# Finishing the last stream in two column runs, gates through tanh, and paired norm additions in a fused layer kernel on eight cores

## The chip, the cores and the metric

The kernel runs on all eight cores of one Trainium2 chip. Cores 0 to 3 are one die, cores 4 to 7 the other. Each core works on one prompt of the batch, with one eighth of the single-token samples, and no core waits for another, so the device time is the time of the slowest core. The metric is that time in microseconds (us). Lower is better.

A program on all eight cores also has a slow state in some of its executions: the cores of one die, sometimes of both, show a lower granted clock (0.81 to 0.98 on them in the slow runs recorded here) and the time is longer (1593 to 1875 us). Engine names in the profile: PE is TensorE, PEld its weight loads, DVE is VectorE, ACT is ScalarE, POOL is GpSimd, SP issues DMA transfers.

## The reference

The reference is one layer of a hybrid decoder, with RMS norms before and after each part:

```
x = x + 0.5 * rms(swiglu1(rms(x)))          # d_model 1024, hidden 2816
h = rms(x);  u = h @ w_in                   # the mixer
  branch A:  (a_b * conv3(a_c * a_x)) @ w_out_a
  branch B:  c = conv4(b_x) + bias
             r = sigmoid(c @ w_r + b_r);  i = sigmoid(c @ w_i + b_i)   # the recurrent gates
             a = exp(-8 * r * softplus(-lambda))
             u = sqrt(1 - a*a) * (i * c);  h_t = a_t * h_(t-1) + u_t
             (gelu(b_gate) * h) @ w_out_b
x = x + rms((sigmoid(g_a)*A + sigmoid(g_b)*B) @ w_o)
x = x + 0.5 * rms(swiglu2(rms(x)))          # the last norm, then the output
```

It returns x for the prompt and the samples, and the new convolution and recurrent states.

## The kernel before

A core keeps features on the 128 partitions and tokens along the columns. Its 2080 tokens are five *streams*. All weights pass through a ring in SBUF once for each group of streams: the first two streams share a pass, the other three have one each.

```python
SIZES = [418, 418, 416, 414, 414]
GROUPS = [[0, 1], [2], [3], [4]]
BUFSET = [0, 1, 2, 0, 1]          # three sets of stream buffers
```

The kernel is written as operations with reads, writes and a priority, and a list scheduler in the program simulates five engines and fixes each engine's order of instructions when the program is built. The priorities come from long tables of fitted numbers, one start and one end for each weight unit of each group. Whoever edits one operation therefore moves many.

```python
def at(g, u, cls, st, fn, *a):
    which, off = CLASSES[cls]
    S.prio = nominal[g][u][which] + off + (LAGS[u] * st.pos if st is not None else 0.0)
    ...
```

A post-norm needs the mean square over features. ScalarE squares each 128-row block as it comes from PSUM, VectorE adds up the squares, and a matmul with a matrix of ones sums over the partitions. The last stream's final norm is then a tail after the last weight matmul:

```python
def rms_finish(ps, n):
    rv = newf()
    act(rv[0:n], ps[0:n], AF.Ln, n, [ps] + DP, [rv], bias=EPS, psum=True)
    act(rv[0:n], rv[0:n], AF.Exp, n, [rv], [rv], scale=-0.5)
    return rv

def final_norm(st, acc):
    s, n, o, m = st.s, st.n, st.o, st.m
    rv = rms_finish(acc, m)
    events = []
    for oc in range(KC):                              # KC = 8 blocks of 128 features
        yv = O32[s][:, oc * m:(oc + 1) * m]           # dense output buffer
        ...
        tt(tv[0:m], y32[s][:, oc, 0:m], rv[0:m], ALU.mult, ...)
        tt(yv, xs_view(st, oc, o, n), tv[0:m], ALU.add, ...)
        if st.last and (oc + 1) % 2 == 0:
            events.append(store_y(st, oc - 1, oc + 1))    # (ACC_TAIL is False)
    return events
```

`xs_view` is the stream's running x in SBUF, `y32` the output of the last product, `O32` a dense fp32 buffer over the hidden activations that are no longer needed. `store_y` sends two blocks, 2 x 414 fp32 values in a row on each partition, in one transfer. The recurrent gates of the mixer take nine ScalarE activations for each stream and block:

```python
act(r, pzr, AF.Exp, scale=-1.0, bias=dcol(0, j));  act(b, pzi, AF.Exp, scale=-1.0, bias=dcol(1, j))
act(r, r, AF.Ln, bias=1.0);  act(r, r, AF.Exp, scale=-1.0);  act(a, r, AF.Exp, scale=dcol(2, j))
act(r, r, AF.Exp, scale=dcol(5, j));  act(r, r, AF.Ln, bias=1.0, scale=-1.0)
act(b, b, AF.Ln, bias=1.0);  stt(r, r, 0.5, b, ALU.mult, ALU.subtract);  act(r, r, AF.Exp)
tt(cb, r, cb, ALU.mult)                      # (slices, reads and writes cut)
```

In the head, `keep_warm(n)` issues matmuls of 128 columns on the ones matrix into a scratch bank; the last 50 of them are the *filler*.

## Time and profile before

| | before |
|---|---|
| median of the first three runs | 1564.75 us (1563.51 to 1565.17) |
| spans of the eight cores in the profiled run | 1557.1 to 1563.7 us |
| TensorE busy, slowest core | 98% |
| last weight matmul to the end, median core | 14.96 us |

The page's first part, kernel before, gives busy time, share of the span and instruction count of each engine:

```profile
span 1563.7 us, 27199 instructions; the slowest of 8 cores (1557.1 to 1563.7 us)
PE 1532.3 (98%) x8771; PEld 847.6 (54%) x8771; DVE 813.1 (52%) x1535; ACT 771.8 (49%) x1367; POOL 247.7 (16%) x470
```

TensorE is the limit, and other engines matter only where TensorE stands still. The view of waits says for what it stood still (total, number of times, longest; the first three lines):

```profile
PE P L662 <- ACT qp L676: 5.9, 5, 3.1
PE P L662 <- DVE qp L680: 3.9, 2, 2.8
PE P L662 <- DVE xs L704: 2.6, 2, 2.2
```

The wait of 2.8 us on `DVE qp` is the third stream's first pre-norm sum, near 78 us. The 2.2 us on `DVE xs` is near 1233 us, in the last stream's mixer. The same two places in the view of windows of core 0; PE's busy time and matmul count come first after the window's length, and the granted clock is the third number from the end:

```profile
76.00:81.00 5.00, 2.17 (x12) 1.07 (x11) 2.88 (x5) 2.58 (x6) 1.05 (x2) 0.95 0.94 176
81.00:84.00 3.00, 3.00 (x10) 1.27 (x9) 0.69 (x2) 2.74 (x4) 0.00 (x0) 0.51 1.03 190
1232.00:1236.00 4.00, 2.43 (x9) 1.17 (x10) 3.42 (x10) 2.83 (x6) 0.42 (x1) 0.78 0.75 258
1236.00:1240.00 4.00, 4.00 (x20) 2.03 (x19) 1.97 (x5) 2.59 (x6) 0.53 (x1) 0.79 0.36 128
```

The tail, in the timeline of core 0 (start, duration, engine, operation; in brackets the idle time before it and what ended it):

```profile
1545.84 2.97 PE L662 MATMUL P<-big,wring 128*128 128x414 bf16 x16
1548.90 0.52 ACT L676 ACTIVATE qp<-P 128x414 bf16<-128x414 f32 x1 [2.64 <-PE P L662]
1549.56 0.34 PE L662 MATMUL P<-qp,ones 128*128 128x414 bf16 x1 [0.58 <-ACT qp L676]
1550.62 0.55 ACT L676 ACTIVATE fp<-fp 128x414 f32<-128x414 f32 x1
1551.27 0.59 DVE L680 TENSOR_TENSOR fp<-hy,fp 128x414 f32<-128x414 f32 x1 [5.01 <-ACT fp L676]
1551.96 0.59 DVE L680 TENSOR_TENSOR big<-xs,fp 128x414 f32<-128x414 f32 x1
...
1560.32 0.59 DVE L680 TENSOR_TENSOR big<-xs,fp 128x414 f32<-128x414 f32 x1
```

The last weight matmul ends at 1548.81. Sixteen VectorE operations run from 1551.27 to 1560.91, and the rest to 1563.7 is the last of four transfers. The DMA view of that stretch:

```profile
GB/s 0 0 0 0 0 0 0 0 0 0 0 0 0 0 0 0 99 397 397 166 0 0 108 389 406 157 0 0 116 397 397 149 0 0 116 397 414 133 0 0
DMA packets 576, 1.70 MB, mean 106 GB/s; under 512 B 64, under 2 KB 64, under 8 KB 576
yout<-big SPq DMA_DIRECT2D x4, 414.0 KB, 2.5
```

Four bursts near 400 GB/s, each over long before the next, so only the last one is waited for.

### The profile page before, as it was taken

The page shows a single profiled execution, that of the slowest core. Times are in us where ns is not written, and L with a number is a line of the kernel's source. Part 1 is how long each engine was busy: PE and PEld are TensorE (multiplying, and loading weights), DVE is VectorE, ACT ScalarE, POOL GpSimd, SP SyncE. Part 2 cuts the span into 40 slices and gives each one's busy share as a digit, 9 for nine tenths or more (in the row PEclk, how much of TensorE's full clock was granted, in tenths as well). Part 3 has the DMA queues.
Part 4 walks back from the last instruction along what each step waited for, and adds up shares of the span by engine and source line. Part 5 has one row for each costly group of instructions (what it writes and reads, how often), then busy time and mean ns, then how long its engine had stood idle before and what let it go on. Part 6 is the DMA issues. An engine that isn't in the chain of part 4 may idle for free.

```text
span 1563.7 us, 27199 instructions; the slowest of 8 cores (1557.1 to 1563.7 us)
## 1 busy us (share of the span) xinstructions
PE 1532.3 (98%) x8771; PEld 847.6 (54%) x8771; DVE 813.1 (52%) x1535; ACT 771.8 (49%) x1367; POOL 247.7 (16%) x470
## 2 busy tenths in 40 slices
PE   8999999999999999999999999999999999999996
PEld 5555555555555555555555555555555555555553
DVE  3232108988787467722127452356567887661143
ACT  3221136788877567411154332446575678451222
POOL 1001111011111111011111122222221111112220
PEclk9999999999999999999999999999999999999998
DMA  9889767766877775898766776655575555545653
GB/s 192 227 193 205 155 159 179 200 146 190 203 162 191 201 201 145 200 203 188 180 178 189 249 247 202 198 181 172 183 254 202 163 174 186 205 170 181 199 185 106
DMA packets 81002, 294.88 MB, mean 189 GB/s; under 512 B 9696, under 2 KB 9824, under 8 KB 80864
## 3 DMA queue, kind: packets, MB, share of 16 engines
q0 software_dynamic: 60704, 223.12, 56.2%
q1 hardware_dynamic: 20160, 70.02, 11.9%
q8 instruction: 74, 1.21, 0.3%
q14 instruction: 64, 0.52, 0.1%
HBM read 284.76 MB, written 64.45 MB: 223 GB/s over the span
## 4 chain that ended last, share of the span: by engine, by line
PE 93%; DVE 3%; DMA 2%; issue 1%; ACT 1%; DVEq 0%; POOL 0%; SPq 0%; ACTq 0%; POOLq 0%
PE P L662 93%; DMA xs<-xin 1%; DMA wring<-wsc 1%; DVE fp L694 1%; DVE fp L680 1%; ACT fp L676 0%; DVE big L680 0%; ACT L676 0%; DVE xs L704 0%; DVE fp L699 0%; DVE fp L688 0%; DVEq L1143 0%; DVE qp L680 0%; ACT qp L676 0%; DVE xs L680 0%
## 5 line engine op out<-in xcount | busy, mean ns | idle before, releaser
L662 PE MATMUL P<-hy,wring 128*128 128x414 bf16 (+4 forms) x6080 | 1101.3, 339 | 5.7 <-DVE xs L704 2.2
L662 PEld LDWEIGHTS P<-hy,wring 128*128 128x128 bf16 x6080 | 591.0, 97 | 487.8 <-issue 14.4
L676 ACT ACTIVATE fp<-P 128x414 f32<-128x414 f32 (+4 forms) x529 | 267.7, 516 | 625.1 <-PE P L662 613.2
L662 PE MATMUL P<-big,wring 128*128 128x414 bf16 (+3 forms) x2400 | 442.8, 338 | 0.3 <-DVE xs L704 0.3
L680 DVE TENSOR_TENSOR big<-P,fp 128x414 bf16<-128x414 f32 (+3 forms) x260 | 151.2, 588 | 403.7 <-PE P L662 379.6
L662 PEld LDWEIGHTS P<-big,wring 128*128 128x128 bf16 x2400 | 233.2, 97 | 189.3 <-issue 1.0
L734 POOL DMA_DIRECT2D wring<-wsc x344 | 182.9, 532 | 802.5 <-PE P L662 786.1
L680 DVE TENSOR_TENSOR fp<-fp 128x414 f32<-128x414 f32 (+3 forms) x215 | 122.5, 572 | 131.2 <-ACT fp L676 124.3
L734 POOL DMA_DIRECT2D wring<-wall x117 | 62.0, 533 | 470.8 <-PE P L662 446.5
L676 ACT ACTIVATE fp<-fp 128x418 f32<-128x418 f32 (+2 forms) x230 | 121.1, 546 | 13.3 <-DVE fp L694 4.0
L676 ACT ACT_TABLE_LOAD x84 | 107.8, 1283 | 28.9 <-PE P L662 19.2
L694 DVE SCALAR_TENSOR_TENSOR fp<-P,par_sb,fp 128x418 f32<-128x418 f32 (+3 forms) x120 | 77.4, 646 | 24.9 <-ACT fp L676 16.9
L694 DVE SCALAR_TENSOR_TENSOR hy<-xs,par_sb,fp 128x414 bf16<-128x414 f32 (+3 forms) x120 | 69.1, 646 | 21.0 <-ACT fp L676 21.0
L694 DVE SCALAR_TENSOR_TENSOR fp<-fp,P 128x414 f32<-128x414 f32 (+3 forms) x80 | 45.4, 580 | 51.6 <-PE P L662 47.5
L676 ACT ACTIVATE fp<-xs 128x414 f32<-128x414 f32 (+3 forms) x104 | 55.1, 545 | 28.2 <-DVE xs L680 27.9
L694 DVE SCALAR_TENSOR_TENSOR fp<-fp,par_sb 128x402 f32<-128x402 f32 (+4 forms) x80 | 51.5, 644 | 7.2
L680 DVE TENSOR_TENSOR fp<-hy,fp 128x414 f32<-128x414 f32 (+3 forms) x80 | 46.7, 584 | 15.6 <-ACT fp L676 15.6
L676 ACT ACTIVATE fp<-fp,dpar 128x418 f32<-128x418 f32 (+2 forms) x80 | 51.1, 639 | 7.2 <-DVE fp L694 1.7
L676 ACT ACTIVATE hy<-P,dpar 128x414 f32<-128x414 f32 (+3 forms) x80 | 48.6, 607 | 7.5 <-ACT fp L676 0.7
L680 DVE TENSOR_TENSOR xs<-xs,fp 128x414 f32<-128x414 f32 (+3 forms) x80 | 47.1, 588 | 6.3 <-DVE fp L680 0.8
L676 ACT ACTIVATE fp<-P,dpar 128x418 f32<-128x418 f32 (+2 forms) x80 | 44.5, 604 | 10.6 <-PE P L662 8.9
L699 DVE TENSOR_TENSOR_SCAN fp<-fp,CAR 128x418 f32<-128x418 f32 (+3 forms) x40 | 43.1, 1076 | 3.8
(44 smaller groups left out, 379.4 us busy)
## 6 DMA issues: line engine op xcount, KB each, us to landing
wring<-wsc POOLq DMA_DIRECT2D x244, 512.0 KB, 4.7
wring<-wall POOLq DMA_DIRECT2D x83, 512.0 KB, 8.2
wsc<-wring SPq DMA_DIRECT2D x83, 512.0 KB, 7.0
wring<-wsc POOLq DMA_DIRECT2D x96, 352.0 KB, 4.1
wring<-wall POOLq DMA_DIRECT2D x32, 352.0 KB, 6.8
wsc<-wring SPq DMA_DIRECT2D x32, 352.0 KB, 5.6
xs<-xin SPq DMA_DIRECT2D x4, 828.0 KB, 7.5
xs<-xin SPq DMA_DIRECT2D x4, 418.0 KB, 6.4
```

What stands on the lines that cost most here:

```text
L662: ins = e.matmul(o, ev(lhs_list[k]), ev(rhs_list[k]), start=(start and k == 0), stop=(stop and k == nk - 1))
L676: return S.op("act", lambda e: e.activation(out=ev(out), in_=ev(in_), func=func, **kw), reads, writes, dur, tbl=TBL.get(func), prio=prio)
L680: return S.op("dve", lambda e: e.tensor_tensor(out=ev(out), in0=ev(in0), in1=ev(in1), op=op), reads, writes, 0.153 + n / 960.0, prio=prio)
L694: return S.op("dve", lambda e: e.scalar_tensor_tensor(out=ev(out), in0=ev(in0), scalar=scalar, in1=ev(in1), op0=op0, op1=op1), reads, writ ...
L699: return S.op("dve", lambda e: e.tensor_tensor_scan(out=ev(out), data0=ev(d0), data1=ev(d1), initial=init, op0=ALU.mult, op1=ALU.add), rea ...
L734: S.dma("pool", lambda e: e.dma_start(out=v[0:n](), in_=rows(src, off, n)), [R_xs(STREAMS[0], 3)] if g == 0 else [("wsc", u)], [v, ("wl", ...
```

## The change

The intent has four parts.

1. **The tail.** The last stream's last two output blocks are computed in two runs of 207 columns, so that the norm and store of the first run can go on under the matmuls of the second. The new final norm writes x in place and stores from there.
2. **The gates.** sigmoid(z) = (1 + tanh(z/2)) / 2 turns nine activations into six.
3. **The norms.** Multiplication and addition of the post-norms handle two blocks in one VectorE instruction.
4. **Fit.** The scheduler's DMA model, a few head operations and all priority tables are fitted anew (144 changed lines of numbers, cut here).

```diff
+TAIL_OC = 6
+TAIL_A = 207
-            act(r[0:n], pzr[0:n], AF.Exp, ...)      # nine activations, cut
+            act(r[0:n], pzr[0:n], AF.Tanh, n, [pzr] + DP, [r], scale=0.5, bias=dcol(0, j), psum=True)
+            act(b[0:n], pzi[0:n], AF.Tanh, n, [pzi] + DP, [b, turn], scale=0.5, bias=dcol(1, j), psum=True)
+            act(a[0:n], r[0:n], AF.Exp, n, [r] + DP, [a], scale=dcol(5, j), bias=dcol(5, j))
+            act(r[0:n], r[0:n], AF.Exp, n, [r] + DP, [r], scale=dcol(2, j), bias=dcol(2, j))
+            act(r[0:n], r[0:n], AF.Ln, n, [r] + DP, [r], bias=1.0, scale=-1.0)
+            act(r[0:n], r[0:n], AF.Exp, n, [r] + DP, [r], bias=cst[:, 1:2], scale=0.5)
+            stt(cb[0:n], b[0:n], 1.0, cb[0:n], ALU.add, ALU.mult, n, [b, cb], [cb])
 # post_norm, and final_norm alike:
-            for oc in range(KC):                     # two instructions of 414 columns each
+            for oc in range(0, KC, 2):
+                tt(src, src, spread(rv[0:m], 2), ALU.mult, 2 * m, res + [rv], res)
+                tt(dst, dst, src, ALU.add, 2 * m, res + dres, dres)
+        def last_norm(st, acc, a, b):
+            s, n, o, m = st.s, st.n, st.o, b - a
+            rv = rms_finish(acc, m)
+            xv = XS[s][:, 0:KC * n].rearrange("p (k t) -> p k t", k=KC)
+            for k0, nk, steps in ((0, 4, 1), (4, 4, 2)):
+                ...multiply four blocks by rv in place...
+                for k1 in range(k0, k0 + nk, nk // steps):
+                    k2 = k1 + nk // steps
+                    yv = xv[:, k1:k2, o + a:o + b]               # 207 columns of each block of x
+                    tt(yv, yv, y32[s][:, k1:k2, a:b], ALU.add, (k2 - k1) * m, ..., [("o32", a, k1)])
+                    dst = yout[:, base:base + (k2 - k1) * m].rearrange("p (k t) -> p k t", t=m)
+                    events.append(S.dma("sp", lambda e, dst=dst, yv=yv: e.dma_start(out=dst, in_=yv),
+                                        [("o32", a, k1)], [], (k2 - k1) * m * 512, stall=0.013))
 # work(), last stream's down-projection:
+                if st.last and not first_ffn and which >= TAIL_OC:
+                    late.append(w)
+                    acc = at(g, u, "work", st, dn_last, st, held[i], which, [half], [w], 0, TAIL_A, sqs[i], sums)
+                    if idx == 15:
+                        at(g, u, "post", st, last_norm, st, acc, 0, TAIL_A)
+                        for oc in range(TAIL_OC, KC):
+                            ...dn_last of columns TAIL_A to st.m...
+                        at(g, u, "post", st, last_norm, st, acc, TAIL_A, st.m)
+                    return
```

## The prediction

> **What bounds it now.** TensorE: the page's first part has PE busy 1532.3 of 1563.7 us (98%); the chain of waits is 93% PE. The windows view of core 0 splits the idle time: 7.8 us in 0-29 (mean clock 0.88), 2.8 in 76-81 (PE waits for the third stream's pre-norm sum), only 6.4 in 81-1548.9, and a tail of 14.8 in which PE does 0.4. ACT or DVE can win only what lies there: 32 us at most.
>
> **Gates through tanh.** Nine ScalarE activations per stream and column block become six. Built, the program has 1166 activations for 1283, but 106 table switches for 84 (counted in program order; the count gives the profile's 84 loads). At 0.54 us an activation and 1.283 a load: -63 + 28, ACT busy 772 to about 737. The Trainium skill, "ScalarE: Activation LUTs", "What ACT_TABLE_LOAD costs", gives 1283 ns a load, as the trace does; its further drain I do not add. ACT is 49% busy: off the critical path, worth 0, +-1.5.
>
> **Paired norm additions.** Two 414-column DVE instructions (0.59 each) become one of 828. "VectorE: DVE Perf Modes", "Why tensor_tensor can't do 2x_2P or 4x", leaves fp32 no faster mode, so only the fixed part is saved: about 0.15 a pair, 17 us of DVE busy (813 to about 797). Worth 0 on the chain.
>
> **The split tail.** Intended: the first half's norm under the second half's matmuls. In the built order this overlap is absent. On PE the last two full-width blocks stand between the halves, and all four 207-column ones-matmuls follow the last weight matmul; ACT does Ln, Ln, Exp, Exp after its last eviction; DVE's ten norm instructions follow. After the last matmul (T), square, copy, two Ln and Exp at 0.35-0.43 each bring DVE to T+2.1 (before 2.46, from 1548.81 to 1551.27); ten DVE instructions, six of about 1.02 and four of 0.59, take 8.5 (before 9.65); the last, smaller store about 2.5 (before 2.8). Tail 13.1 for 14.9. On PE 44 full matmuls become 88 of 207 columns: 88 x 0.09-0.097 against 44 x 0.175, +0.2 to +0.8. Net -1.2, where a true overlap would give about -6.
>
> **Head.** Table loaded early, half the squares on DVE, Ln no longer behind the parameter chain: the first normalised column starts about 0.9 earlier, but PE still waits for the second stream's load (landing 20.9). About -1.
>
> **New order of work.** The third stream's ones-matmul comes after 224 instead of 272 matmuls, its eight squares in one run; its input lands at about 61 us and PE gets there at 68: the 2.8 us stall should go. Other stalls (2.2 before the last stream's mixer, 1-3 of weight waits) may go or be replaced: -1 +-2.
>
> **Sum.** 1564.75 - 1.2 - 1 - 2.8 - 1 = about 1558.8 us; 8 in 10: 1552.5 to 1563.5. Faster by over 2%: 0.01; within 2%: 0.98; slower by over 2%: 0.01.
>
> **Signs.** Right: 106 table loads, ACT about 737, DVE about 797, PE 98%; 12.5-13.7 us from the last 207-column weight matmul to the end, the first half's DVE multiplication starting only after it; no 2.8 us PE wait near 77. Wrong: output stores of the last stream landing while weight matmuls run (true overlap, then nearer 1554); PE waits on ACT in the mixers beyond 8 us (table switches on the path); 207-column matmuls well over 0.1 us.
>
> **What would spoil it.** The landing of the second and third streams' inputs and the half-rate clock in the head, which already make cores differ by 6 us; one badly placed ones-matmul in the new order.

## The result, and the profile after

| | before | after |
|---|---|---|
| median | 1564.96 us (1563.51 to 1565.91, 4 runs) | 1563.64 us (1563.11 to 1565.52, 4 runs) |
| ratio of fast runs | | 0.9995, 95% interval 0.9977 to 1.0012 |

A ratio in this document is the measuring program's, over the fast runs of both kernels in the same rounds, so it is not quite the ratio of the medians quoted beside it. The predicted gain of 6 us is not there: 1563.64 lies just outside the predicted range of 1552.5 to 1563.5.

Where the time went is best read as marks along each core's trace. The table gives the median of the eight cores of the profiled run for each mark. The medians of parts do not add up exactly.

| median of eight cores, us | before | after | moved |
|---|---|---|---|
| start of the 50 filler matmuls (head) | 24.08 | 24.28 | +0.2 |
| filler to the end of the last weight matmul | 1522.63 | 1514.73 | -7.9 |
| last weight matmul to the end of the last VectorE operation | 12.11 | 11.42 | -0.7 |
| from there to the end (the last store) | 2.86 | 7.33 | +4.5 |
| span | 1562.25 | 1559.05 | -3.2 |

Two large movements of opposite sign. The middle is 7.9 us shorter, where the prediction summed to some 3 to 4. The store after the last operation costs 4.5 us more, where the prediction had it slightly shorter. In this profile the stores are longest on die 0 (8.6 to 9.7 us; 5.2 to 6.1 on die 1), so the slowest core keeps less of the gain than the median core. It is no property of a die: in two later kernels with small pieces die 1 had the longest stores (up to 13.5 and 12.4 us).

The page's first part, after, and the table loads of both kernels from the view of groups (before first):

```profile
span 1561.7 us, 26950 instructions; the slowest of 8 cores (1551.6 to 1561.7 us)
PE 1530.1 (98%) x8817; PEld 851.1 (54%) x8817; DVE 801.8 (51%) x1422; ACT 753.2 (48%) x1272; POOL 247.6 (16%) x470
```

```profile
L676 ACT ACT_TABLE_LOAD x84 | 107.8, 1283 | 28.9 <-PE P L662 19.2 <-DMA xs<-xin 5.2 <-DVE big L680 2.3
```

```profile
L675 ACT ACT_TABLE_LOAD x106 | 136.0, 1283 | 30.1 <-PE P L661 24.1 <-DVE big L679 2.1 <-DVE cstcol L711 1.7
```

The windows view after, core 2, where the third stream's sum comes: no wait, and no slow clock behind it. In 81 to 84 us there are 19 matmuls, not 10.

```profile
76.00:81.00 5.00, 5.00 (x30) 2.74 (x29) 1.27 (x3) 1.12 (x3) 0.00 (x0) 1.00 1.07 205
81.00:84.00 3.00, 3.00 (x19) 1.62 (x18) 0.59 (x1) 0.52 (x1) 0.00 (x0) 1.00 0.99 176
```

The tail, timeline of core 2, where the last weight matmul ends at 1541.50:

```profile
1539.33 2.68 DVE L679 TENSOR_TENSOR fp<-fp 128x414 f32<-128x414 f32 x4 [4.78 <-ACT fp L675]
1542.75 0.63 PE L661 MATMUL P<-qp,ones 128*128 128x207 bf16 x4 [1.25 <-DVE qp L679]
1543.22 0.59 ACT L675 ACTIVATE fp<-P 128x207 f32<-128x207 f32 x2 [0.76 <-PE P L661]
1543.90 0.69 ACT L675 ACTIVATE fp<-fp 128x207 f32<-128x207 f32 x2
1544.38 1.02 DVE L679 TENSOR_TENSOR hy<-hy,fp 128x828 f32<-128x828 f32 x1 [1.61 <-ACT fp L675]
...
1546.74 6.70 SPq L852 DMA_DIRECT2D yout<-xs  x6
...
1551.82 1.09 DVE L679 TENSOR_TENSOR xs<-xs,hy 128x414 f32<-128x414 f32 x2
```

There is no overlap: all four ones-matmuls, both Ln, both Exp and all norm operations come after the last weight matmul, as the prediction read from the built order. The ten norm operations take 1544.38 to 1552.91, 8.53 us. But then the core runs on to 1561.7. The DMA view says why:

```profile
GB/s 0 0 0 0 0 0 0 0 0 15 0 0 0 12 343 193 95 113 110 102 108 98 108 107 104 86 116 110 132 152 206 184 200 200 154 63 2 0 0 0
DMA packets 2146, 1.71 MB, mean 78 GB/s; under 512 B 96, under 2 KB 2144, under 8 KB 2144
q1 hardware_dynamic: 2144, 1.70, 60.2%
yout<-xs SPq DMA_DIRECT2D x2, 414.0 KB, 7.7
yout<-xs SPq DMA_DIRECT2D x4, 207.0 KB, 8.2
```

The same 1.70 MB, in 2144 packets under 2 KB in place of 576. The first burst runs at 343 GB/s, nearly as fast as before; then the rate falls to about 100 GB/s for 7 us, the transfers run into each other, and the median transfer lands 7.7 or 8.2 us after its issue. One packet's mean time is the queue's share times the window times 16 engines over the packets: 0.602 x 22 us x 16 / 2144 = 99 ns. But no such time belongs to a packet of 828 bytes. Core 4, with the same instructions, in the view of 1534 to 1553 us:

```profile
GB/s 0 0 0 0 0 0 0 0 0 0 17 0 0 0 0 0 316 347 247 197 262 204 152 72 49 314 312 209 202 223 181 185 99 17 0 0 0 0 0 0
q1 hardware_dynamic: 2144, 1.70, 36.6%
```

That is 0.366 x 19 us x 16 / 2144 = 52 ns a packet. In the packed trace the 828-byte packets of the first half microsecond took 40 ns on either core, where the 3312-byte packets of the kernel before took 131 ns, so four times the bytes took about three times as long. From 1 us after the first packet core 2's took 115 to 180 ns on average for some 7 us, single ones up to 491 ns. The means of the eight cores are 54 to 103 ns. So small pieces are nearly as fast as large ones at first and then slow down.

### The profile page after: what moved, and what is told of

It reads as the page before. It is cut to its first block, busy times and chain, and to the rows that moved or that the text cites. A ratio compares the mean times of both kernels' runs of the same rounds, so it can differ in the third digit from the quotient of the medians.

```text
span 1561.7 us, 26950 instructions; the slowest of 8 cores (1551.6 to 1561.7 us)
## 1 busy us (share of the span) xinstructions
PE 1530.1 (98%) x8817; PEld 851.1 (54%) x8817; DVE 801.8 (51%) x1422; ACT 753.2 (48%) x1272; POOL 247.6 (16%) x470
## 3 DMA queue, kind: packets, MB, share of 16 engines
q1 hardware_dynamic: 21440, 70.02, 12.4%
## 4 chain that ended last, share of the span: by engine, by line
PE 91%; DMA 4%; DVE 2%; issue 1%; ACT 1%; DVEq 0%; POOL 0%; ACTq 0%; POOLq 0%; SPq 0%
PE P L661 91%; DMA wring<-wall 2%; DMA xs<-xin 1%; DVE fp L693 1%; DMA wsc<-wring 1%; ACT fp L675 0%; DVE fp L679 0%; DVE big L679 0%; DVE hy L679 0%; DMA wring<-wsc 0%; DVE fp L698 0%; DVE xs L679 0%; ACT L675 0%; ACT qp L675 0%; DVEq L1182 0%
## 5 line engine op out<-in xcount | busy, mean ns | idle before, releaser
L661 PE MATMUL P<-hy,wring 128*128 128x414 bf16 (+5 forms) x6080 | 1093.6, 338 | 5.3 <-DMA wring<-wall 1.8
L661 PE MATMUL P<-big,wring 128*128 128x414 bf16 (+4 forms) x2444 | 439.8, 335 | 0.0
L661 PEld LDWEIGHTS P<-big,wring 128*128 128x128 bf16 x2444 | 236.9, 97 | 185.5 <-issue 0.4
L679 DVE TENSOR_TENSOR fp<-fp 128x414 f32<-128x414 f32 (+4 forms) x215 | 122.8, 573 | 190.9 <-ACT fp L675 181.9
L675 ACT ACT_TABLE_LOAD x106 | 136.0, 1283 | 30.1 <-PE P L661 24.1
L675 ACT ACTIVATE fp<-xs 128x414 f32<-128x414 f32 (+3 forms) x104 | 50.8, 541 | 26.5 <-DVE xs L679 21.4
L675 ACT ACTIVATE fp<-fp,dpar 128x418 f32<-128x418 f32 (+2 forms) x80 | 58.5, 731 | 5.4 <-DVE fp L679 0.9
L675 ACT ACTIVATE hy<-P,dpar 128x414 f32<-128x414 f32 (+4 forms) x82 | 49.0, 597 | 7.2
L679 DVE TENSOR_TENSOR big<-big,fp 128x414 bf16<-128x414 bf16 (+7 forms) x60 | 42.9, 727 | 17.9 <-ACT fp L675 14.2
L675 ACT ACTIVATE fp<-P,dpar 128x418 f32<-128x418 f32 (+2 forms) x80 | 44.1, 605 | 11.0 <-PE P L661 10.7
L679 DVE TENSOR_TENSOR hy<-hy,fp 128x828 f32<-128x828 f32 (+3 forms) x40 | 40.6, 1015 | 14.2 <-ACT fp L675 14.2
L675 ACT ACTIVATE fp<-P,par_sb 128x418 f32<-128x418 f32 (+2 forms) x40 | 27.8, 694 | 28.6 <-PE P L661 27.5
```

What stands on the lines that cost most here:

```text
L661: ins = e.matmul(o, ev(lhs_list[k]), ev(rhs_list[k]), start=(start and k == 0), stop=(stop and k == nk - 1))
L675: return S.op("act", lambda e: e.activation(out=ev(out), in_=ev(in_), func=func, **kw), reads, writes, dur, tbl=TBL.get(func), prio=prio)
L679: return S.op("dve", lambda e: e.tensor_tensor(out=ev(out), in0=ev(in0), in1=ev(in1), op=op), reads, writes, 0.153 + n / 960.0, prio=prio)
```

## The experiments

Fourteen kernels ran. Times are medians of the fast runs. Marks are medians of eight cores as in the table above.

### Store the split tail from a dense buffer

The split, its order and everything else stay. The additions write to the dense buffer of an idle stream set, from which 828-byte pieces of neighbouring blocks are adjacent.

```diff
+            ov = O32[2][:, KC * a:KC * b].rearrange("p (k t) -> p k t", k=KC)
+            free = [R_hid(c, 2) for c in range(16)]
-                    yv = xv[:, k1:k2, o + a:o + b]
-                    tt(yv, yv, y32[s][:, k1:k2, a:b], ALU.add, ...)
+                    yv = ov[:, k1:k2, :]
+                    tt(yv, xv[:, k1:k2, o + a:o + b], y32[s][:, k1:k2, a:b], ALU.add, ... + (free if k1 == 0 else []))
```

> The changed kernel with one thing different: the last stream's normalised columns are written to a dense buffer (that of the third stream, long free), so each store reads one run of 1656 or 3312 bytes a partition in place of pieces of 828. Order and number of all instructions stay. Theory S (the small pieces slow the store): the time from the last norm addition to the end falls from 5.2-9.7 us by core (median 7.3) to about 3, as before the change, and the median time falls by 3 to 6 us, to about 1559. Rival P (the store is slow because 1.7 MB of all cores is now stored in a shorter stretch): the store time stays over 5 us and the median within 1 us of 1563.6.

Measured: 1561.25 us, ratio 0.996 (0.9941 to 0.998), a gain somewhat under the 3 to 6 us expected. VectorE still ends 11.91 us after the last weight matmul, and the store falls from 7.33 to 2.73 us. From the DMA view of this kernel:

```profile
DMA packets 867, 1.73 MB, mean 115 GB/s; under 512 B 96, under 2 KB 608, under 8 KB 864
yout<-big SPq DMA_DIRECT2D x2, 414.0 KB, 2.4
yout<-big SPq DMA_DIRECT2D x4, 207.0 KB, 2.0
```

Landing is back at 2.0 to 2.4 us. In the packed trace the packets of 1656 bytes take 70 to 71 ns and those of 3312 bytes 130 to 131 ns on every core (means), and none of the slow-down is left. All eight cores store the same bytes here in the same stretch, so it needs the small pieces. The whole excess of the store was the shape of its source. With that one thing removed, the time lies inside the predicted range.

### The kernel before, with small pieces

The converse: the kernel before, its last four stores split into eight with 207 columns a piece.

```diff
+            if st.last:
+                h = m // 2
+                for a in (0, h):
+                    d_ = yout[:, a0 + KC * a + k0 * h:a0 + KC * a + k1 * h].rearrange("p (k t) -> p k t", t=h)
+                    s_ = src.rearrange("p (k t) -> p k t", t=m)[:, :, a:a + h]
+                    out.append(S.dma("sp", lambda e, d_=d_, s_=s_: e.dma_start(out=d_, in_=s_), ...))
```

> The kernel before, its last stream's four stores cut in column halves, so that each reads pieces of 828 bytes from the on-chip buffer (eight issues in place of four, the same bytes, the same arithmetic). Theory S: at the 110 GB/s seen after the change, 1.7 MB take some 15 us from the first issue, so the end comes 5 to 6 us later, about 1570. Rival P: the additions still spread the stores over 10 us, so within 1 us of 1565.

Measured: 1573.10 us, ratio 1.0039 (1.0023 to 1.0055). VectorE's part is unchanged at 12.11 us and the store takes 8.75. In the DMA view:

```profile
yout<-big SPq DMA_DIRECT2D x8, 207.0 KB, 7.2
```

Its 828-byte packets took 104 ns on average on this core (61 to 128 ns over the cores), in a kernel without any split arithmetic. On core 0 the first six of its eight stores still ran at 38 to 43 ns a packet, and the slow-down came with the last two. The cost of small pieces is shown from both sides; what starts the slow-down is not.

### The overlap made real, with small pieces and with the dense buffer

Why was there no overlap? In the changed kernel the fourth stream's final norm stands on VectorE before the last stream's sums, and the tables let both full-width last blocks run on PE between the two halves. The edit sorts the last sixteen table entries, puts the fourth stream's norm in a late class, and gives the tail's stores a key of their own (the old key collides with one of the fourth stream's).

```diff
+for _t in (STARTS, ENDS):
+    _t[3][-16:] = sorted(_t[3][-16:])
+           "late": (1, 3000.0),
-                       [("o32", a, k1)]
+                       [("tail", a, k1)]
-                    at(g, u, "post", st, final_norm, st, acc)
+                    at(g, u, "late" if st.i == 3 else "post", st, final_norm, st, acc)
```

> The changed kernel with the overlap made real, its stores left in pieces: the last stream's sixteen down-projection units take sorted priorities, so both 207-column runs come last; the third stream's final norm takes a lower priority than the last stream's sums; a name shared by mistake between the first run's results and another stream's buffer is made separate. Theory O (the order kept the first run's norm from lying under the matmuls): the last norm addition ends some 6.5 to 8 us after the last weight matmul in place of 11.4. Under theory S the small pieces then hold the end, some 15 us after the first store of this stream: median about 1560. If S is wrong and only the order matters: about 1558.

(The "third stream" of this text has index 3; it is the fourth.)

Measured: 1564.25 us, ratio 0.9985 (0.997 to 0.9999), 4 us above the expected 1560. VectorE now ends 9.16 us after the last weight matmul and the first store is issued 3.5 us before it, but the tail is still 20.7 us: the DMA queue, not the arithmetic, ends the program. Overlap gains nothing while the store is the chain.

With both edits, the dense buffer and the order:

> Both edits together, dense stores and the real order. S and O both right: last addition 6.5 to 8 us after the last weight matmul, store about 3, tail about 10 us for 18.8 (median of cores), median time about 1554. If either is wrong, at or above 1558.

Measured: 1557.69 us, ratio 0.9939 (0.9924 to 0.9954). The tail is 12.30 us (9.29 + 3.01). It beats both kernels. Its VectorE works without a gap of more than 0.24 us from well before the last weight matmul to the end, because the fourth stream's postponed norm runs there too. So 9.3 us and not the hoped-for 6 to 7.

### No split at all

The changed kernel with the last stream at full width again.

```diff
-TAIL_OC = 6
+TAIL_OC = 8
+                    for k0 in (0, 2, 4, 6) if st.last else ():
+                        out_events.append(at(g, u, "post", st, store_y, st, k0, k0 + 2))
```

> The changed kernel with its last stream finished at full width again: gates, priorities and pairs as changed, but one run of 414 columns, four stores of dense pairs of blocks as before. It is meant to be read against the dense-buffer run of the split (ratio 0.9960, about 1561 us; last weight matmul to last VectorE operation 11.91 us, store 2.73, together 14.6). If the split as it was built hides nothing, because both full-width last blocks stand between its halves: the last weight matmul comes about 0.7 us earlier (64 fewer 207-column starts), the VectorE part is about 10.7, the store 2.9, the tail 13.6, and the time about 1560, ratio 0.995 to 0.996: the split is worth nothing or costs 1 us, and all of the gain is the order and the gates. If the split did pay once its store was dense: tail 16 or more and a time of 1563 or more.

Measured: 1559.69 us, ratio 0.9966 (0.9952 to 0.998), against 0.996 for the split with the dense buffer. Filler to last weight matmul is 1514.72 us (1516.21 there), the tail 14.78 (14.63). I expected 10.7 us for VectorE's part and it is 11.92: the norms now start 3.25 us after the last weight matmul, 0.8 later than before, since VectorE must add up the last squares before the ones-matmul, and the pairs give back no more than that. (The 64 starts in the expectation should be 44, 88 narrow matmuls for 44 wide ones.) The main expectation holds: the split, as built, is worth nothing.

### Half of the postponed norm on GpSimd

The best kernel, with the fourth stream's last four blocks normalised on GpSimd to relieve VectorE, and the last norms in the late class.

```diff
+        def tt_pool(out, in0, in1, op, n, reads, writes):
+            return S.op("pool", lambda e: e.tensor_tensor(out=ev(out), in0=ev(in0), in1=ev(in1), op=op), reads, writes, 2.0)
+                t2 = tt_pool if st.i == 3 and oc >= 4 else tt
```

> The best kernel so far (dense store, last stream's first half normalised under the second half's matmuls; 1557.69, ratio 0.9939), with the second half of the fourth stream's final norm moved from VectorE to GpSimd, because VectorE was busy without a gap from before the last weight matmul to its last operation. If VectorE's throughput is what ends the tail: last weight matmul to last VectorE operation 6.5 to 7 in place of 9.3 us, the tail 9.5 to 10, the time about 1555. Against: GpSimd's operations may take several us each and slow VectorE's own while they run; then the tail stays at 12 or grows, and the time is 1558 or more.

Measured: 1562.04 us, ratio 0.9976 (0.9962 to 0.999): slower than the best kernel. The tail did shrink to 9.30 us, as hoped, but filler to last weight matmul grew from 1515.51 to 1523.79. Timeline of core 1, VectorE and then GpSimd:

```profile
1537.16 2.19 DVE L684 TENSOR_TENSOR fp<-fp 128x414 f32<-128x414 f32 x1
1539.27 2.75 DVE L684 TENSOR_TENSOR big<-xs,hy 128x828 f32<-128x828 f32 x1
1544.47 2.10 DVE L684 TENSOR_TENSOR qp<-fp 128x207 bf16<-128x207 f32 x1
```

```profile
1536.27 2.63 POOL L814 TENSOR_TENSOR hy<-hy,fp 128x828 f32<-128x828 f32 x1 [10.51 <-ACT fp L680]
1539.04 2.10 POOL L814 TENSOR_TENSOR big<-xs,hy 128x828 f32<-128x828 f32 x1
1543.81 2.52 POOL L814 TENSOR_TENSOR big<-xs,hy 128x828 f32<-128x828 f32 x1
```

While GpSimd works, a VectorE addition of 414 columns takes 2.19 us in place of 0.58, and the 207-column sum for which PE waits takes 2.10 in place of 0.37. PE stood still for 5.5 us waiting for that sum. This agrees with the Trainium skill, "SBUF — State Buffer", section "SBUF: two separate sides", which describes an exclusive lock on a shared port pair between GpSimd and a VectorE operation with two SBUF inputs, where the other "fully blocks": in this trace the 828-column addition at 1539.27 ends at 1542.02, 0.88 us after the GpSimd operation that it met, and alone it takes 1.01.

### The gates and the pairs

The dense-buffer kernel with its 80 Tanh instructions issued twice, the first time into a junk tile:

```diff
-            act(r[0:n], pzr[0:n], AF.Tanh, ...);  act(b[0:n], pzi[0:n], AF.Tanh, ...)
+            act_more(r[0:n], pzr[0:n], AF.Tanh, ..., 1, ...);  act_more(b[0:n], pzi[0:n], AF.Tanh, ..., 1, ...)
```

> The dense-store version, with each gate's two Tanh activations issued twice (the first result thrown away), 80 more activations in the same order, so that most of the ScalarE time that the change took out of the gates is put back: busy 753 to about 797 us. Prediction (off the chain): filler-to-last-matmul time within 1 us of 1516, median within 1.5 us of 1561. Rival G: waits in the mixers grow and it is 2 us or more slower.

Measured: 1563.56 us, ratio 0.9992 (0.9979 to 1.0004). ScalarE's busy time went from 753.7 to 786.9 us and filler to last weight matmul from 1516.2 to 1519.5. PE's idle time between 250 and 450 us, the first mixer, went from 2.9 to 6.2. So 33 us of gate work cost 3.3 us in this order: the prediction's "off the critical path, worth 0" does not hold in the first mixer of the changed kernel.

The other way round, in the kernel before: three of the nine gate activations shrunk to one column. The output is wrong (relative error 0.83).

```diff
-            act(r[0:n], r[0:n], AF.Ln, n, [r] + DP, [r], bias=1.0)
+            act(r[0:n], r[0:n], AF.Ln, n, [r] + DP, [r], bias=1.0, short=True)      # and two more
```

> The kernel before in its own order, but three of the nine ScalarE activations of each gate block shrunk to one column (wrong result on purpose): ScalarE loses about 40 us of busy time, some 22 us more than the change itself takes away. Theory that the gates pay only through waits of TensorE in the first mixer: TensorE idles 1.7 us at 250 to 450 us of the kernel before, so the stretch from the first filler matmul to the last weight matmul loses at most 2 us (1522.6 to about 1521) and the time at most 2 us, ratio 0.9985 to 1.000. Rival, the gates explain the 7 to 8 us by which the changed kernel's same stretch is shorter: ratio 0.995 or less. If the third-stream stall near 78 us and the waits at 1000 to 1300 us stay (2.8 and 3.0 us), they belong to the order and not to the gates.

Measured: 1564.86 us, ratio 1.000 (0.9986 to 1.0014). ScalarE lost 38 us, PE's idle time stayed (9.2 to 9.6 us in all, 1.74 to 1.74 in the first mixer). From filler to last weight matmul it took 1521.60 us, as expected. Cheaper gates alone gain nothing in the old order. Their gain, if any, needs the order that uses it.

The dense-buffer kernel with each pair issued as two instructions:

```diff
+                for k in range(2):
+                    ins = e.tensor_tensor(out=ev(out)[:, k, :], in0=ev(in0)[:, k, :], in1=ev(in1)[:, k, :], op=op)
```

> The dense-store version, each paired norm instruction of 828 columns of the first four streams and of the inner norms issued as two of 414, in the same place of the same order. Vector busy time rises by about 16 us. If the pairing is off the chain (prediction): filler-to-last-matmul time within 1 us of 1516 and the median within 1.5 us of 1561. Rival G: 2 us or more slower.

Measured: 1558.97 us, ratio 0.9964 (0.995 to 0.9977), against 0.996 with the pairs. VectorE's busy time rose by 6.2 us (802.0 to 808.2) for 112 pairs, 0.055 us a pair, a third of the predicted 0.15. Pairing moves no time.

### Order of work: two kernels that failed

The dense-buffer kernel with the priority tables of the kernel before:

```diff
-LAGS, STARTS, ENDS, CLASSES      # as fitted for the change (numbers cut)
+LAGS, STARTS, ENDS, CLASSES      # as in the kernel before
```

> The dense-store version of the changed kernel, with the priorities of the kernel before (all of its tables of starts, ends, lags and classes), so the new code stands in an order made from the old priorities. Theory Q (the new order, not the gates or the paired norms, made the matmul part shorter): the time from the head's last filler matmuls to the last weight matmul, 1522.6 us before and 1514.7-1516.2 after (medians of cores), returns to 1519-1523, and the run is 3 to 6 us slower than the dense-store version (1561). Rival G (the cheaper gates and norms did it): it stays at 1514-1517 and the median within 1.5 us of 1561.

Measured: 1580.06 us, ratio 1.0092 (1.0079 to 1.0105). PE idles 19.6 us between 30 and 1530 us. The tables are fitted to the code they were made for, so this run shows that order alone can move the time by some 19 us (1561.25 to 1580.06). It is far more than the 3 to 6 us expected, and it does not show what the change's order is worth over the old one on equal terms. (The converse, the old code with the new tables, did not build: the scheduler deadlocked.)

The best kernel with the fourth stream's down-projection 200 units earlier in priority, to get its norm out of the tail:

```diff
+    _t[2][-16:] = [x - 200.0 for x in sorted(_t[2][-16:])]
```

> The version with dense stores and real order (1557.7), and the fourth stream's down-projection moved earlier by priority, so that its final norm is done before the last stream's runs of 207 columns. There the vector engine was busy without a pause from 4 us before the last norms to the end, with two of the fourth stream's four norm pairs among them. If that held the end: the last addition 6.3 to 7 us after the last weight matmul in place of 9.3, tail 9.0 to 9.8 us in place of 12.3, median 1554 to 1556. If the matmul part suffers from the moved priorities, the filler-to-last-matmul time shows it (1515.5 in the version without).

Measured: 1580.74 us, ratio 1.0093 (1.0079 to 1.0108). PE idles 15.8 us between 1300 and 1530, mostly waiting for weights (9.1 us on the profiled core). It failed, and only shows that the postponed norm can't be had out of the way by moving that block alone.

### Why the middle shrank by 7.9 us

PE's idle time between 30 and 1534 us fell from 9.23 to 4.37 us (median core), which explains 4.9 of 7.9. In 2-us windows of that stretch I then added up the busy time multiplied by what the granted clock lacked, where it was below 0.97: **3.20 us in the kernel before, 0.00 in the changed one**. 4.86 + 3.20 is 8.1, the whole movement in these two profiles. (The end of this section shows that the 3.20 is a high draw.)

In the kernel before, the low clock stands only behind its two long waits. The 2.83 us near 78 us were followed by a dip on seven cores of eight (1.4 to 1.7 us lost on each), the 2.2 us near 1233 also on seven of eight. Waits of 0.9 to 1.5 us were never followed by one. But both waits always came at the same stage, so a wait and its surroundings could not be told apart. Three kernels do that.

The first fills the wait near 78 us in the kernel before with 30 matmuls into the bank that the waiting matmul overwrites:

```diff
+                if st.i == 2 and gvi == 0:
+                    S.ops[i].fill = lambda e: [e.matmul(ev(ps[0:128]), ones[:, :], ones[:, :], start=True, stop=True)
+                                               for _ in range(FILL)]
```

> The kernel before, its own order, with 30 matmuls of 128 columns added into the 2.83 us wait of TensorE for the third stream's pre-norm sum (written into the very PSUM bank that the waiting matmul overwrites, and thrown away). In the kernel before, seven of eight cores show a granted clock near one half for 3 to 4 us after that wait, 1.4 to 1.7 us of work lost on each. Theory, that a wait of that length itself brings the clock down: with matmuls in the wait none of the eight cores shows a dip at 76 to 88 us, the stretch from filler to last weight matmul is about 1 us shorter (1522.6 to about 1521.3), the other wait at 1233 us keeps its dip in most cores. Rival, the dip comes from this stage (its DMA load, its VectorE work) and not from the idleness: most cores still show it. The time moves by too little to be told, ratio 0.998 to 1.001.

Measured: 1563.57 us, ratio 0.9985 (0.9968 to 1.0003). The remaining wait is 1.16 us on every core and none of the eight shows a dip. Filler to last weight matmul is 1519.05 us, 3.6 less than before, more than the 1.3 expected: the other wait, untouched at 2.21 us, was followed by a dip on only two cores this time. In the kernel with small gates, which has the same two waits, it was four and four; in the kernel before with small pieces, six and three. Whether a wait of 2.2 to 2.8 us is punished differs from run to run.

The other two put four waits on PE where there were none, near 130, 190, 560 and 620 us of the dense-buffer kernel. PE waits for a chain of three, or nine, tiny ScalarE operations that starts when PE arrives.

```diff
+        for p, v in at_pe:
+            prog["pe"][p] = ([("stl", v)] + prog["pe"][p][0],) + prog["pe"][p][1:]
+        for i, (a, v) in reversed(list(enumerate(at_act))):
+            prog["act"][a:a] = [
+                (([("pe", v)] if r == 0 else []) + ([("stl", i * DELAY + r)] if i + r else []), self.delay, ("stl", 1))
+                for r in range(DELAY)]
```

> The dense-buffer kernel with four waits of about 1.3 us put on TensorE in stages where it never waits (near 130, 190, 560 and 620 us): TensorE waits for a chain of three tiny ScalarE operations that start when it arrives. Theory, waits under about 1.5 us cost only themselves: 4 x 1.3 = 5 us more from filler to last weight matmul (1516.2 to about 1521.5), no dip of the clock after them on any core, ratio to before about 0.9995. Rival, every wait costs the clock too: 8 us or more.

Measured: 1566.30 us, ratio 1.0001 (0.9981 to 1.0021). (The time verdicts on this kernel and the next are "unclear"; what is read is the profiles.) Waits of 1.12 to 1.32 us, filler to last weight matmul 1521.76 (+5.6), idle time +5.2, and no dip in any of the 32 places.

> As the run before it, with chains of nine tiny operations, for four waits of about 2.8 us. Theory, waits over about 2.2 us are followed by 3 to 4 us at half clock on most cores: 4 x 2.8 = 11.2 us of waiting and about 4 x 1.2 = 5 us of slow matmuls behind them, 16 us in all from filler to last weight matmul (1516.2 to about 1532), dips in at least 20 of the 32 places, ratio to before about 1.0065. Rival, a wait costs itself: 11 us, 1527, ratio 1.003.

Measured: 1578.60 us, ratio 1.0082 (1.0062 to 1.0102). Waits of 2.96 to 3.16 us, filler to last weight matmul 1533.31 (+17.1): idle time +11.6 and 4.7 us lost to the clock, with a dip in 25 of 32 places. One of them, core 6, in the timeline of PE and the windows:

```profile
204.43 1.90 PE L675 MATMUL P<-big,wring 128*128 128x418 bf16 x5 [2.96 <-ACT dly L1196]
```

```profile
196.00:201.00 5.00, 5.00 (x30) 2.73 (x29) 0.00 (x0) 1.13 (x2) 1.06 (x2) 1.00 1.06 149
201.00:204.00 3.00, 0.46 (x3) 0.04 (x1) 0.00 (x0) 1.72 (x8) 0.53 (x1) 0.95 1.02 238
204.00:206.00 2.00, 1.57 (x5) 0.74 (x6) 0.00 (x0) 0.21 (x1) 0.00 (x0) 0.50 1.03 392
```

Five matmuls in 1.57 us behind the wait, where the same shape runs at six a microsecond elsewhere. So a wait itself brings the clock down, and it depends on its length: 1.3 us costs 1.3, 3.0 us costs about 4.3 (17.1 / 4, with the four waits' effects taken together).

Length is not all of it, and the packed traces hold the rest. Each trace records when the granted clock changed. Every stretch at half clock is one, two or three pieces of 3.41 us, and on each core of the sixteen kernels all of them, the head's and the tail's too, begin whole multiples of 3.4133 us apart (core 0 of the kernel before: 80.55 and 1234.25 us, 338 steps). So each core has a fixed grid of 3.41 us, which doesn't start with a wait. Core 0 and core 3 of the kernel before, cut along their own grids, with the same wait of 2.83 us:

```profile
77.14:80.55 3.41, 0.58 (x4) 0.27 (x3) 2.85 (x5) 1.25 (x3) 1.05 (x2) 1.00 0.95 178
80.55:83.96 3.41, 3.41 (x12) 1.51 (x10) 0.67 (x3) 3.01 (x4) 0.00 (x0) 0.50 0.96 173
```

```profile
73.70:77.11 3.41, 1.56 (x9) 0.66 (x7) 1.64 (x3) 2.27 (x5) 1.05 (x2) 1.00 1.00 195
77.11:80.52 3.41, 2.43 (x14) 1.44 (x15) 1.23 (x3) 1.85 (x3) 0.00 (x0) 1.00 0.76 118
```

On core 0 the whole wait fell into one piece of the grid (PE busy for 0.58 of 3.41 us) and the next piece ran at half clock. On core 3 it was split, 1.85 and 0.98 us idle, and nothing followed. All sixteen kernels and eight cores, from about 27 to 1533 us, have 56,225 pieces at full clock. In 85 of them TensorE was idle for 2.0 us or more in all, and 83 of these were followed by a piece at half clock; of the other 56,140, three were (1.80 us idle each, all in the kernel with the earlier down-projection). So in these traces a wait is punished when it puts about 2.0 us of idleness into one piece. A wait of 1.3 us can't. For the others an estimate from where they may fall on the grid is 48% at 2.2 us, 66% at 2.83 and 71% at 3.0; counted over all kernels with these waits it is 16 of 32, 17 of 24 and 25 of 32.

It also says that the profile of the kernel before was unlucky, with 14 dips in 16 places. The two kernels with the same order and the same two waits lost 1.67 (small pieces) and 1.61 us (small gates) to the clock, not 3.20, and took 1521.0 and 1521.6 us from filler to last weight matmul. Of the 7.9 us some 1 to 1.6 is this draw.

## Why the prediction was right or wrong

**The step that failed** is the tail's last term: "the last, smaller store about 2.5 (before 2.8)". It took its size from the bytes of the last store. Measured: 7.33 us on the median core, 5.2 to 9.7 over the cores. The transfer is smaller in bytes, but its source is x in place, rows of 207 fp32 values with other columns between them, and so in 828-byte packets. These started at about 340 GB/s and then fell to about 100 (core 2; why is open), and six such stores queue behind each other. The tail was predicted at 13.1 us and measured at 18.75. The dense-buffer run (store 2.73, time 1561.25) and the kernel before with small pieces (store 8.75) show it from both sides.

**Right in the tail:** no overlap in the built order, 8.53 us for the ten VectorE operations (predicted 8.5), and 207-column matmuls at 8.4 us for 88, 0.095 each (predicted 0.09 to 0.097). The norms began 2.88 us after the last weight matmul on core 2 and not 2.1, since VectorE was late with the last sums. What the narrow matmuls cost PE beyond that can't be told: from filler to last weight matmul the run at full width is 1.5 us below the dense-buffer run and level with the changed kernel (1514.72, 1516.21 and 1514.73).

**A second error, of opposite sign:** "the 2.8 us stall should go" and other stalls "-1 +-2". The stalls went, as predicted. But each was sized by its idle time, and the slow clock behind it was left out: 3.2 us on the median core of this profile, about 1.6 in two others. Together -7.9 in place of about -3.3 (-2.8, -1 and +0.5 for PE's narrow matmuls). The data was there: the windows of the kernel before show a clock of 0.51 from 81 to 84 us. With the predicted -3.3 in the middle, the head's +0.2 and the tail's +3.8, the median core would have been no faster than before. That the median of the runs came within 0.2 us of the predicted range is luck: one error hid most of the other.

**The head:** -1 predicted, +0.2 measured. The first normalised column was to start 0.9 us earlier; it started 0.7 later (14.98 us for 14.24, medians of cores, which range from 13.7 to 16.3 after the change). What holds the head was not taken apart.

**Gates:** 106 table loads, as predicted, at the 1283 ns that the Trainium skill gives ("ScalarE: Activation LUTs", "What ACT_TABLE_LOAD costs"). ScalarE's busy time was 753, not 737: the count of activations was right but the two Exp with both scale and bias read from memory take about 730 ns, where the old ones with a scale alone took 640, and the one with a bias column about 640. The same section of the skill states it: each such operand adds about 93 ns. The prediction had counted 0.54 us for every activation; these two groups are about 11 of the 16 us. "Worth 0" held in the old order (38 us removed, nothing gained) and not in the new (33 us added, 3.3 lost).

**Pairs:** no effect on the time, as predicted. A pair saves 0.055 us and not 0.15, because two independent instructions overlap: they start 0.51 us apart though each lasts 0.59. VectorE's busy time was 802 and not 797; the pairs make up 6.2 of the 11 us that it fell, and where the rest comes from was not looked into.

**Cores:** the sum of medians, -3.2 us, is not the device's gain, -1.3. The slowest core is one with a long store.

What stays open: how much of the -7.9 us is owed to the new tables and how much to the tables' being able to use the cheaper gates; and what makes 828-byte packets slow down after a fast start, at a different moment on each core. The cores' traces have no common clock, so whether other cores' stores at the same time set it off can't be read from them.

## What to carry to other kernels

Before you move a store earlier, look at how many contiguous bytes each of its rows has: a store in place from a column slice can cost more than the overlap gains, and an idle dense buffer is often there. Size a wait of TensorE by what follows it too: a stretch that is "busy" at half the granted clock behind a wait of over 2 us belongs to that wait, and removing or filling the wait gives it back, as the filled wait near 78 us shows. When a scheduler with fitted priorities decides the order, read overlap from the built order of each engine, and don't count the gain of one edit until the others are fitted to it.

## What the Trainium skill lacked or had wrong

- "TensorE: Matmul & The Clock Gate", section "Why this matters for your kernels", advises no PE-idle gaps above about 3 us, and "What's actually happening" has the array cold after one idle window of about 3.4 us. Here a window need not be idle throughout: 2.0 us of idleness in one was enough in 83 of 85 cases. So single waits of 2.2 us were followed by half clock in 16 of 32 places, of 2.83 us in 17 of 24 and of 3.0 us in 25 of 32; single waits up to 1.9 us never. Each dip cost 1.2 to 1.7 us in most cases. The page says that the window runs freely and is 3413 ns long, and the traces' clock records agree: half clock starts on a grid of 3.4133 us on every core.
- "DMA: Bandwidth & Descriptors", section "Why small descriptors are slow (HBM only)", gives a fixed overhead of about 3 cycles a packet (27% at 256 bytes), which would be an estimated 10% at 828 bytes. Here packets of 828, 1656 and 3312 bytes took 39, 69 and 131 ns (medians, 828 bytes in the first burst), so the smallest were 19% above a quarter of the largest. What made the stores slow is not on the page: within about a microsecond the 828-byte packets went to 115 to 180 ns on core 2, and those of 1656 and 3312 bytes stayed as they were on every core.
- "SBUF — State Buffer" is right about the lock between VectorE and GpSimd but has no size for a tensor_tensor beside a tensor_tensor: a 207-column addition that met a GpSimd addition of 2.52 us took 2.10 us in place of 0.37.
